# First input transfer of a dilated convolution issued from ScalarE's queue, beside the weights on SyncE's

## The chip, the cores and the metric

The kernel runs on one core of a Trainium2 chip. The metric is the device time of one execution in microseconds (us). A profiled execution gives in addition the span from the first to the last instruction, and the time of each instruction and each DMA packet. The engines are TensorE (PE, with its weight loads as PEld), VectorE (DVE), ScalarE (ACT), GpSimd (POOL) and SyncE (SP); transfers are issued from SyncE's and ScalarE's instruction queues and carried by 16 DMA engines. In the profile, q1 is the DMA queue that SyncE issues to and q10 the one that ScalarE issues to.

## What is computed

A 3x3 convolution with dilation 2 over 16 images of 64 channels, 64 by 64, to 128 output channels, zero padded so that the output is 64 by 64 too.

```python
x_pad = np.pad(x, ((0, 0), (0, 0), (2, 2), (2, 2)))
for kh in range(3):
    for kw in range(3):
        output[b, co] += weight[co, ci, kh, kw] * x_pad[b, ci, kh*2:kh*2+64, kw*2:kw*2+64]
```

Inputs, weights and output are float32: 16.8 MB of input, 0.3 MB of weights and 33.6 MB of output.

## The kernel before

The work goes by pairs of images. A pair has the 64 channels of one image on partitions 0 to 63 and those of the other on 64 to 127, so an input tile (`x32`, line 64) is 128 partitions by 4096 elements. There are eight pairs, and each is worked off in four groups of 16 output rows: 32 groups in all, in one order written out by hand (the loop over `G`).

Row blocks are combined before they are multiplied, so that fewer products are needed: in each group TensorE makes three sets of matmuls (line 173), `psP` from sums of rows (`xs`), and `psA` and `psB` from the rows themselves (`x16`, half precision), against five kinds of weights that are prepared from the three rows of the filter. A group has 6 + 12 + 12 matmuls. ScalarE then copies `psP` out of PSUM (`p_sb`, line 225), and VectorE adds it to `psA` and to `psB` (line 232) into the output tile `osb`.

Around these, by line:

- **Loads.** `load` (line 61 on) makes a tile of three buffers and issues its transfers (line 64). At the start SyncE issues the weights (line 88, 288 KB), then pair 0 in two pieces, rows 0 to 33 (1088 KB) and rows 34 to 63 (960 KB), then pairs 1 and 2 whole (2048 KB each). The loads of pairs 3 to 7 are issued by ScalarE, each after the last cast of the pair whose buffer it takes.
- **Weights.** When they have landed, VectorE, GpSimd and ScalarE make the five kinds (`wd`, lines 111 to 115). TensorE turns them with an identity matrix (line 124), and VectorE and ScalarE copy them out of PSUM as `w_sb` (lines 134 to 148). In ScalarE's queue stand, in this order: the copy to `wd` (113), the copy of kind 1 (136), the cast of rows 0 to 7 of pair 0 (146), the copy of kind 3 (147), then `casts(0)`: three casts of pair 0 (line 73: rows 18 to 33, 34 to 49, 50 to 63) and the load of pair 3, and then the first copy of `psP` (225). VectorE casts rows 8 to 17 (143) after its copy of kind 2 (138).
- **Dummies.** Ten matmuls on zeros (line 101) are placed between the steps of the preparation.
- **PSUM.** `psP` has one buffer, so the `psP` of the second group begins when the first has been copied out. `psA` and `psB` share three.
- **Stores.** SyncE issues them (line 186), each image of a pair on its own: pairs 0 and 7 in halves of 32 rows (1024 KB each, eight in all), pairs 1 to 6 whole (2048 KB, twelve in all). `osb` has three buffers, so pair n writes where pair n-3 stood, once its stores have landed.

```python
    w32 = wpool.tile([CO, CI * KH * KW], f32, name="w32")
    nc.sync.dma_start(out=w32, in_=weight.rearrange("o i h w -> o (i h w)"))
    load(0, (0, 2 * GR + d, H))
    load(1)
    load(2)
```

Here `GR` is 16, `d` is 2 and `H` is 64. Tiles and their waits are handled by the framework; the order of instructions on each engine is that of the code. The functions, with the line numbers of the profile:

Of the kernel before, what the change touches and what calls it, by code (L numbers as in the profile page):

```python
# [10 lines left out]
def kernel(  # L11
# [7 lines left out]
    nc = tc.nc  # L19

    B, CI, H, W = x.shape
# [5 lines left out]
    d = 2  # L27
# [8 lines left out]
    GR = 16  # L36
# [17 lines left out]
    x_pair = x.rearrange("(nb two) c h w -> nb (two c) (h w)", two=2)  # L54
# [4 lines left out]
    x32_tiles, x16_tiles, xs_tiles, o_tiles = {}, {}, {}, {}  # L59

    def load(pb, cuts=(0, H), queue=nc.sync):
        x32_tiles[pb] = fpool.tile([P, HW], f32, tag="x32", name="x32")
        for lo, hi in zip(cuts[:-1], cuts[1:]):
            queue.dma_start(  # L64
                out=x32_tiles[pb][:, lo * W : hi * W], in_=x_pair[pb, :, lo * W : hi * W]
            )
# [18 lines left out]
        nc.vector.tensor_tensor(out=s, in0=v[:, :, 0], in1=v[:, :, 1], op=add)  # L85

    w32 = wpool.tile([CO, CI * KH * KW], f32, name="w32")
    nc.sync.dma_start(out=w32, in_=weight.rearrange("o i h w -> o (i h w)"))  # L88
    load(0, (0, 2 * GR + d, H))
    load(1)  # L90
    load(2)
    zero = wpool.tile([P, 512], f16, name="zero")
# [26 lines left out]
    def turn(k):  # L119
# [24 lines left out]
        out=x16_tiles[0][:, 8 * W : 18 * W], in_=x32_tiles[0][:, 8 * W : 18 * W]  # L144
# [46 lines left out]
    for G in range(ngroups):  # L191
# [39 lines left out]
        for e, ps in ((0, psA), (1, psB)):  # L231
            nc.vector.tensor_tensor(  # L232
                out=o[:, :, b0 : b0 + NBLK, e],
# [49 lines left out]
```

## Time and profile before

| what | value |
|---|---|
| time, median of 8 runs | 127.63 us (127.17 to 128.65) |
| the profiled execution | 127.69 us, span 125.9 us |
| PE busy | 105.5 us (84%) |
| DVE busy | 90.5 us (72%) |
| ACT busy | 65.0 us (52%) |
| moved by DMA | 50.78 MB, mean 403 GB/s over the span |
| DMA time of SyncE's queue (q1) | 75.7% of 16 engines' span |
| DMA time of ScalarE's queue (q10) | 19.9% of 16 engines' span |
| instruction fetches (q8) | 8 packets, 0.13 MB |

The page lists each transfer that is issued, with its size and the median time from issue to landing. For the start of the kernel these lines matter (columns: what, engine, count, KB each, us to landing):

```profile
x<-in_x_dram SPq DMA_DIRECT2D x2, 2048.0 KB, 17.2
x<-in_x_dram SPq DMA_DIRECT2D x1, 1088.0 KB, 5.5
x<-in_x_dram SPq DMA_DIRECT2D x1, 960.0 KB, 7.3
w<-in_weight_dram SPq DMA_DIRECT2D x1, 288.0 KB, 2.9
```

A busy share is an average over the span. Matmuls are pipelined, so a busy PE is not one at its peak. In the slices of the span each digit is a share in tenths, and a slice is 3.15 us long. A line of the timeline gives start, length, engine, source line, operation, the tiles written and read, and in brackets how long the engine stood idle before it and who released it.

### The profile page before, as it was taken

Reading aid. Unit: us, or ns where it says so; the run is one execution under the profiler, and the core shown is the slowest. Engines: PE = TensorE matmul, PEld = TensorE weight load, DVE = VectorE, ACT = ScalarE, POOL = GpSimd, SP = SyncE. Lnnn points to the kernel's source line nnn. Section 1 sums busy time; section 2 is a strip of 40 time slices with the busy share of each in tenths; the row PEclk is TensorE's granted clock in tenths of the full one; section 3 lists DMA queues with packets and bytes.
Section 4 is the critical chain, followed back from the end, with each engine's and each line's share of the span. In section 5 each row is a group of like instructions: output and inputs, shape, how many; then the busy total and the mean of one; then the engine's idle time right before and its main releaser. Section 6 shows DMA issues by size and latency. Waiting matters only on the chain.

```text
span 125.9 us, 2336 instructions
## 1 busy us (share of the span) xinstructions
PE 105.5 (84%) x1000; PEld 54.1 (43%) x1000; DVE 90.5 (72%) x103; ACT 65.0 (52%) x68; POOL 2.2 (2%) x8
## 2 busy tenths in 40 slices
PE   6994999999999999999999995999999999900000
PEld 2251555555555555555555552445444444400000
DVE  0560998988898888988988827999888988740000
ACT  4287794366656665666666665566666533300000
POOL 2400000000000000000000000000000000000000
PEclk9999999999999999999999999999999999997555
DMA  4999999999999999999999999999999999999960
GB/s 134 374 439 427 442 422 390 390 424 409 427 432 437 427 432 432 435 416 411 427 435 432 427 427 427 432 427 442 427 416 432 427 427 442 427 393 432 432 273 26
DMA packets 4330, 50.78 MB, mean 403 GB/s; under 512 B 480, under 2 KB 480, under 8 KB 736
## 3 DMA queue, kind: packets, MB, share of 16 engines
q1 hardware_dynamic: 3600, 40.14, 75.7%
q10 hardware_dynamic: 720, 10.49, 19.9%
q8 instruction: 8, 0.13, 0.4%
q14 instruction: 2, 0.02, 0.0%
HBM read 17.07 MB, written 33.55 MB: 402 GB/s over the span
## 4 chain that ended last, share of the span: by engine, by line
PE 76%; DMA 6%; DVE 2%; ACT 2%; issue 1%; DVEq 1%; SPq 1%; ACTq 0%
PE psA L173 30%; PE psB L173 29%; PE psP L173 16%; DMA x<-in_x_dram 6%; DVE osb L232 2%; DVEq L278 1%; ACT p_sb L225 1%; ACT x L73 1%; SPq L64 0%; ACTq L64 0%; SPq L88 0%; DVEq L232 0%
## 5 line engine op out<-in xcount | busy, mean ns | idle before, releaser
L173 PEld LDWEIGHTS <-w_sb 64*128 64x128 f16 x960 | 52.0, 94 | 51.0 <-issue 3.9
L225 ACT COPY p_sb<-psP 128x1024 f32<-128x1024 f32 x32 | 32.4, 1012 | 39.3 <-PE psP L173 20.1
L232 DVE TENSOR_TENSOR osb<-psA,p_sb 128x1024 f32<-128x1024 f32 x32 | 39.2, 1224 | 16.3 <-PE psA L173 11.7
L173 PE MATMUL psB<-x,w_sb 64*128 64x496 f16 (+3 forms) x384 | 44.9, 365 | 1.4 <-DVE osb L232 1.4
L173 PE MATMUL psA<-x,w_sb 64*128 64x496 f16 (+3 forms) x384 | 44.9, 365 | 0.1
L232 DVE TENSOR_TENSOR osb<-psB,p_sb 128x1024 f32<-128x1024 f32 x32 | 39.1, 1220 | 0.0
L73 ACT CAST x<-x 128x1024 f16<-128x1024 f32 (+2 forms) x31 | 32.1, 1044 | 0.4 <-DMA x<-in_x_dram 0.4
L173 PE MATMUL psP<-xs,w_sb 64*128 64x496 f16 (+1 forms) x192 | 25.9, 371 | 1.9 <-ACT p_sb L225 1.9
L85 DVE TENSOR_TENSOR xs<-x 128x512 f16<-128x512 f16 x32 | 13.3, 416 | 0.7 <-ACT x L73 0.7
L101 PE MATMUL dm<-zero 128*128 128x512 f16 x10 | 4.6, 578 | 1.2 <-DVE zero L93 1.2
L111 DVE CAST wd<-w 128x192 f16<-128x192 f32 x1 | 0.5, 505 | 2.5 <-DMA w<-in_weight_dram 2.5
L101 PEld LDWEIGHTS <-zero 128*128 128x128 f16 x10 | 1.0, 122 | 2.7 <-issue 1.3
L124 PEld LDWEIGHTS <-wd 128*64 128x64 f16 x30 | 1.0, 118 | 2.3 <-DVE wd L111 1.2
L124 PE MATMUL wt<-ident,wd 128*64 128x128 f16 x30 | 1.6, 241 | 0.3 <-DVE wd L111 0.3
L113 ACT ACT_TABLE_LOAD x1 | 1.3, 1283 | 0.7 <-PEq L264 0.7
L136 ACT CAST w_sb<-wt 128x384 f16<-128x384 f32 x1 | 0.5, 479 | 1.9 <-PE wt L124 1.9
L113 ACT CAST wd<-w 128x192 f16<-128x192 f32 x1 | 0.5, 542 | 1.6 <-DMA w<-in_weight_dram 1.6
L138 DVE CAST w_sb<-wt 128x384 f16<-128x384 f32 x1 | 0.6, 558 | 0.9 <-PE wt L124 0.9
L93 DVE MEMSET zero<- 128x256 uint32 x1 | 0.3, 272 | 0.9 <-PEq L264 0.9
L112 POOL TENSOR_TENSOR wd<-w 128x192 f16<-128x192 f32 x1 | 0.8, 799 | 2.4 <-DMA w<-in_weight_dram 2.4
L115 POOL CAST wd<-w 128x192 f16<-128x192 f32 x1 | 0.8, 809 | 0.0
L114 DVE TENSOR_TENSOR wd<-w 128x192 f16<-128x192 f32 x1 | 0.8, 792 | 0.0
(11 smaller groups left out, 3.6 us busy)
## 6 DMA issues: line engine op xcount, KB each, us to landing
out_dram<-osb SPq DMA_DIRECT2D x12, 2048.0 KB, 18.9
x<-in_x_dram ACTq DMA_DIRECT2D x5, 2048.0 KB, 15.2
out_dram<-osb SPq DMA_DIRECT2D x8, 1024.0 KB, 14.7
x<-in_x_dram SPq DMA_DIRECT2D x2, 2048.0 KB, 17.2
x<-in_x_dram SPq DMA_DIRECT2D x1, 1088.0 KB, 5.5
x<-in_x_dram SPq DMA_DIRECT2D x1, 960.0 KB, 7.3
w<-in_weight_dram SPq DMA_DIRECT2D x1, 288.0 KB, 2.9
```

Of the source, the lines that this page charges most:

```text
L73: nc.scalar.copy(out=x16_tiles[pb][:, lo * W : hi * W], in_=x32_tiles[pb][:, lo * W : hi * W])
L85: nc.vector.tensor_tensor(out=s, in0=v[:, :, 0], in1=v[:, :, 1], op=add)
L101: nc.tensor.matmul(out=dm[:, 0:512], lhsT=zero[:, 0:P], rhs=zero)
L112: nc.gpsimd.tensor_tensor(out=wdv[:, 3], in0=wv[:, 0], in1=wv[:, 1], op=sub)
L113: nc.scalar.copy(out=wdv[:, 2], in_=wv[:, 0])
L114: nc.vector.tensor_tensor(out=wdv[:, 1], in0=wv[:, 2], in1=wv[:, 1], op=sub)
L115: nc.gpsimd.tensor_copy(out=wdv[:, 4], in_=wv[:, 2])
L124: nc.tensor.matmul(out=wts[k % 3][r * CI : (r + 1) * CI, c0 + j * CO : c0 + (j + 1) * CO], lhsT=wd[:, t * CI : (t + 1) * CI], rhs=ident,)
L173: nc.tensor.matmul(out=po, lhsT=w_sb[pp, t * CO : (t + 1) * CO], rhs=rhs, start=first and j == 1, stop=last and j == 2,)
L225: nc.scalar.copy(out=p_sb, in_=psP)
L232: nc.vector.tensor_tensor(out=o[:, :, b0 : b0 + NBLK, e], in0=ps.rearrange("p (m b q) -> p m b q", m=2, q=2 * W), in1=pv, op=add,)
L278: with _tile.TileContext(nc) as tc:
```

## The change

The first piece of pair 0 (rows 0 to 33) is issued by ScalarE as its first instruction, ahead of its table load and of everything else in its queue. SyncE issues the weights, then the second piece (rows 34 to 63), then pairs 1 and 2. Sizes, tiles and all other instructions stay as they were. In the order of instructions on the engines, ScalarE has one transfer more at its head and SyncE one fewer after the weights; TensorE, VectorE and GpSimd have theirs in the same order.

```diff
     w32 = wpool.tile([CO, CI * KH * KW], f32, name="w32")
+    load(0, (0, 2 * GR + d), queue=nc.scalar)
     nc.sync.dma_start(out=w32, in_=weight.rearrange("o i h w -> o (i h w)"))
-    load(0, (0, 2 * GR + d, H))
+    nc.sync.dma_start(
+        out=x32_tiles[0][:, (2 * GR + d) * W :], in_=x_pair[0, :, (2 * GR + d) * W :]
+    )
     load(1)
     load(2)
```

## The prediction

> **What bounds the kernel now.** I read first the page's row of engines and its slices of the span, to see which resource is full.
>
> ```profile
> PE 105.5 (84%) x1000; PEld 54.1 (43%) x1000; DVE 90.5 (72%) x103; ACT 65.0 (52%) x68; POOL 2.2 (2%) x8
> DMA  4999999999999999999999999999999999999960
> GB/s 134 374 439 427 442 422 390 390 424 409 427 432 437 427 432 432 435 416 411 427 435 432 427 427 427 432 427 442 427 416 432 427 427 442 427 393 432 432 273 26
> ```
>
> TensorE is busy in most slices and idle in the last five; the DMA row is full from the second slice to the thirty-eighth. Stretches of the trace say the same more finely (columns: stretch, its length, busy time and count of PE, PEld, DVE, ACT and POOL, clock, DMA share, GB/s).
>
> ```profile
> 1.00:2.00 1.00, 0.81 (x2) 0.28 (x3) 0.13 (x1) 1.00 (x1) 0.29 (x1) 1.00 0.23 30
> 2.00:3.00 1.00, 1.00 (x4) 0.42 (x3) 0.00 (x0) 0.02 (x1) 0.00 (x0) 1.00 1.04 343
> 12.40:75.00 62.60, 62.60 (x608) 34.65 (x609) 54.47 (x60) 39.15 (x40) 0.00 (x0) 1.00 1.01 423
> 115.00:121.00 6.00, 0.00 (x0) 0.00 (x0) 0.00 (x0) 0.00 (x0) 0.00 (x0) 0.50 1.00 422
> 121.00:126.00 5.00, 0.00 (x0) 0.00 (x0) 0.00 (x0) 0.00 (x0) 0.00 (x0) 0.50 0.19 80
> ```
>
> The DMA engines start at 1.74 us (first packet record), are full from 2 us, and still empty a backlog of stores when every engine has stopped (last add ends at 111.67). Can one engine's own packets explain its whole time? Each transfer has 128 rows, one packet each, 8 on each of 16 engines. Median packet: weights (2304 bytes) 93 ns, first piece (8704) 328, second (7680) 291, a 16384-byte row 611, an 8192-byte row 309. Per engine: 8 x (93 + 328 + 291) = 5.7; seven full loads and twelve full stores, 19 x 8 x 0.611 = 92.9; eight half stores, 64 x 0.309 = 19.8; sum 118.4 us. From 1.74 that ends at 120.1, and the first engine's part of the last store lands at 121.04. The last lands at 124.96, because two engines, judging by the landings, also carry the eight instruction fetches (886 to 964 ns each, four per engine is 3.7): 1.74 + 118.4 + 3.7 + 0.36 (last weights packet ended 3.28, landed 3.64) = 124.2, against 124.96. So the slowest DMA engine has at most some 0.8 us of slack in the whole run. The end is set by bytes on an engine that never runs dry.
>
> The chain of waits, next, seems to say otherwise. Columns: start, length, what.
>
> ```profile
> 1.64 7.33 DMA x<-in_x_dram
> 9.94 0.94 ACT x L73
> 10.90 0.39 ACTq L64
> 11.33 1.02 ACT p_sb L225
> 12.40 0.81 PE psP L173 x6
> 109.31 1.23 DVE osb L232
> ```
>
> It follows instructions and ends with VectorE's last add, not with the stores. Its start matters, though: TensorE stands from 10.52 to 12.40 for the first eviction (L225), which is queued on ScalarE behind two casts of rows 34 to 63. And its middle holds one stall, which shows who leads.
>
> ```profile
> 76.46 1.23 DVE L232 TENSOR_TENSOR osb<-psA,p_sb 128x1024 f32<-128x1024 f32 x1 [3.37 <-PE psA L173]
> 77.74 1.44 PE L173 MATMUL psB<-x,w_sb 64*128 64x512 f16 x12 [1.42 <-DVE osb L232]
> ```
>
> TensorE stops for 1.42 us because pair 5's output buffer is pair 2's, and pair 2's last store lands at 76.27 on the slowest DMA engine. Compute had run ahead of the stores and waits for them here: a start up to 1.4 us later is taken back at this point.
>
> **The change, part by part.** Three parts.
>
> *One issue leaves SyncE, one enters ScalarE.* SyncE's issue of 0.42 us (L64, from 1.17) goes; the second piece and pairs 1 and 2 are issued 0.47 us earlier, behind a queue that is full anyway. ScalarE issues first: 0.39 us by its own L64 row, then its table load of 1.28 us, now from about 1.1 to 2.4 instead of 0.73 to 2.01. Its next work needs the weights, at 3.66 at the earliest. Covered; uncovered it would be 0.4 us. GpSimd's queue issues nothing. No semaphore wait is added.
>
> *Start of the DMA.* The Trainium skill (DMA: Bandwidth & Descriptors, "Issuing engines are not separate DMA queues") holds that queues share the same 16 engines, so a second issuer saves only the sequencer's issue time. By that rule the gain is 0.42 us. By the rows it is nothing: the first piece's issue ended at 1.59 and its first packet came at 2.69, behind the weights on engines already full. The first packet of all stays 1.0 us after SyncE's issue at 0.74. What could shrink is the ramp: the weights' packets took 122 ns in the mean against 93, the first piece's 374 against 328, together 8 x (29 + 46) = 0.6 us. Bounds: 0.6 us less, or as much more; I take 0, since the same bytes start on the same idle engines.
>
> *The weights now share the engines.* Before, they were alone and landed at 3.64. How the queues share is seen from 24 to 30 us, where q1 carries 8192-byte rows and q10 16384-byte rows (columns: packets, MB, share):
>
> ```profile
> q10 hardware_dynamic: 114, 1.80, 70.8%
> q1 hardware_dynamic: 101, 0.75, 29.4%
> ```
>
> Packets alternate about one for one, whatever their size. The same skill page ("Queues, rings and completion order") agrees on round robin but puts some 9 to 17 descriptors in a packet; then an engine's 8 weight rows would pass as one, undelayed or behind all 8 rows of x: 0 or 8 x 0.328 = 2.6 us later. By the row, 8 pairs of 93 + 328 ns take 3.4 us: 1.74 + 3.4 + 0.36, with some ramp, is about 5.6, so +2.0 us. I take +2.0 and keep 0 and +2.7. The first piece lands near 5.7 to 6.6 (before 6.64) and no longer binds.
>
> All that hangs on the weights moves by 2.0: the wd copies 3.66 to 5.7, the casts of rows 0 to 17 from 6.66 to 8.7, first psA 7.33 to 9.3, end of the first psP 10.52 to 12.5. Queued on ScalarE behind the first wd copy: the w_sb copy, the x cast, the second w_sb copy, three casts, the load of pair 3, the eviction. Before, the last two casts waited 0.39 us for the second piece (8.97); that wait vanishes, since the piece lands as before, the bytes ahead of it being the same. So the casts end at 8.60 + 2.0 + 1.89 = 12.5, the issue of pair 3's load at 12.9, and the first eviction starts at 12.9 instead of 11.33: **+1.6 us** for TensorE (0 if the weights go first, 2.3 if x does). By the page's packets it would be 0 or 2.3.
>
> **What is late next.** TensorE runs without a gap from 12.4 to 75, so every store moves by 1.6. That costs only if a DMA engine runs dry. The tightest point is pair 1's first store, issued at 35.68. The engines finish the stores ahead of it between 38.0 and 41.1 (landings 38.31 to 41.48, less 0.36). With 1.6 us of delay and 1.0 us to the first packet it is there at 38.3: the quickest engines stand for 0.3 us, and they finish 3.9 us before the last one at the end. The slowest two finish their earlier stores at 39.6 and 41.1 and have 1.3 us or more to spare. At 76 the delay shrinks to 0.2. At 99.3, the next tight point, the quickest engines have 0.8 us of backlog beyond the 1.0; at 111.7 over 4. Sum for the slowest engine: 0. The profiled execution took 127.69, 1.8 outside its span; the median is 127.63. I forecast **127.6**.
>
> **The rivals.**
>
> *Compute sets the end.* Then +1.6 would arrive: 129.2. Against it: 10 us of full DMA after the last add, and the stall at 76. This needs two facts to be wrong; 0.03.
>
> *Slower: the new queue starts late and the DMA runs dry.* ScalarE's loads at 10.90, 36.89, 49.26 and 61.63 had their first packets at 14.46, 40.52, 52.85 and 65.42, 3.6 us or more after issue. If the first is that late too, x's packets start near 4.3, alternate with the second piece and pair 1, and land near 10.7; the cast at 6.66 slips by 4.0 and the first eviction to about 15.2, +3.9. TensorE would also stand some 4 us, and at the end its clock fell from 1.00 to 0.50 about 4.6 us after its last matmul; half clock over the 3.2 us of the first group adds up to 3.2. It decides once the delay passes 2.9: the second slowest engine, free at 39.6, then waits for 35.68 + delay + 1.0. At 3.9 it idles 1.0 and ends 0.8 after the old end: 128.4; at 7 several us later. Against it: those four issues met full engines, and this one meets idle ones, as SyncE's at 0.74 did (1.0 us to the first packet). The stall in the likeliest case is 2.3 us (3.93 to 6.2), nearer to the 1.9 at 10.52, after which the clock stood at 1.00. 0.15.
>
> *Faster: two queues fill the ramp.* Up to 0.6 us less, 127.0; a part of it, 127.3, is well possible but below what can be told. Over 0.5% needs more than the whole ramp: 0.06.
>
> *It does not do what it says:* the weights pass undelayed, compute starts as before, 127.6 again; it counts with the forecast.
>
> **How the numbers follow.** The forecast with its neighbours has 0.76, the first two rivals 0.18, the faster one 0.06. A measurement of this kernel can tell about 0.5%, 0.64 us, from no change: below 127.0 is faster, above 128.3 slower. The range goes from 127.0, the ramp gone, to 128.6, the late queue without a clock drop. The likeliest case's own range is 127.2 to 128.0.
>
> **What would show it.** Right: the weights land near 5.6, the wd copies start there, the first eviction near 12.9, the stall at 76 shrinks to about 0.2 us, the last add ends within 0.3 us of 111.7, the last store lands near 125, DMA share stays 1 from 2 to 121 us. Wrong: weights at 3.6 (then the sharing step fails, not the sum); a DMA share under 0.9 near 38 us; the first packet off 1.74; a last add over 2 us later.

## The result, and the profile after

The changed kernel takes 130.02 us in the median of 11 runs (128.79 to 130.96); the kernel before takes 127.69 us in 32 runs. The ratio is 1.0155, 95% interval 1.0127 to 1.0183: slower by 1.55%. The ratio leaves out runs more than 1.5% above the quickest of their kernel, so it is a little under the quotient of the medians. The profiled execution took 129.17 us (span 127.4), so it is one of the quicker ones; a second profile, further down, took 130.25.

The slices of the page, with the row of the granted clock this time:

```profile
PEclk9968999999999999999999999999999999975555
DMA  3999999999998999999999999999999999999981
GB/s 59 431 446 427 437 427 417 401 432 404 386 391 368 345 386 427 442 373 437 442 414 406 432 432 427 427 432 427 432 427 422 432 432 422 422 422 422 424 365 44
```

The clock is down in parts of the third and fourth slices, the DMA row has an 8 in the thirteenth (38.2 to 41.4 us), and the rates of the eleventh to the fifteenth are 345 to 391 GB/s. The same start in the timeline:

```profile
6.18 0.54 ACT L116 CAST wd<-w 128x192 f16<-128x192 f32 x1 [3.72 <-DMA w<-in_weight_dram]
6.74 0.36 PE L127 MATMUL wt<-ident,wd 128*64 128x128 f16 x6 [2.81 <-DVE wd L114]
9.10 0.85 PE L127 MATMUL wt<-ident,wd 128*64 128x128 f16 x12
10.42 1.40 PE L176 MATMUL psA<-x,w_sb 64*128 64x512 f16 x12
13.77 1.01 ACT L228 COPY p_sb<-psP 128x1024 f32<-128x1024 f32 x1 [0.88 <-PE psP L176]
```

The weights land at 6.15 us instead of 3.64, TensorE stands 2.81 us before them, its turn of twelve weight tiles takes 0.85 us instead of 0.53, and the first eviction (the copy of `psP`) starts at 13.77 instead of 11.33: 2.4 us late. It waits for `psP` now, no longer for the casts ahead of it in ScalarE's queue. In the kernel before:

```profile
6.43 0.53 PE L124 MATMUL wt<-ident,wd 128*64 128x128 f16 x12
7.33 1.29 PE L173 MATMUL psA<-x,w_sb 64*128 64x512 f16 x12
```

Stretches of the span (columns as before: length, busy time and count of PE, PEld, DVE, ACT, POOL, clock, DMA share, GB/s):

```profile
2.00:3.00 1.00, 1.00 (x4) 0.43 (x3) 0.00 (x0) 0.46 (x1) 0.00 (x0) 1.00 0.52 100
37.00:38.00 1.00, 1.00 (x13) 0.56 (x11) 1.00 (x2) 0.55 (x1) 0.00 (x0) 1.00 0.84 352
38.00:39.00 1.00, 1.00 (x14) 0.62 (x12) 0.83 (x3) 1.00 (x2) 0.00 (x0) 1.00 0.68 287
43.00:44.00 1.00, 1.00 (x12) 0.52 (x10) 1.00 (x1) 0.41 (x1) 0.00 (x0) 1.00 1.13 262
```

TensorE is busy all through 37 to 44 us, and the DMA is not: pair 1's first store is issued at 38.11 (before: 35.68), when the engines have little left. The last line shows something else: engines full, but only 262 GB/s. Packets of 16384 bytes took up to 1.2 us instead of 0.61. From the packet records I use two sums, each a mean over the 16 DMA engines, for every run: idle time from 15 to 50 us (35 us less the time of all data packets over 16, and 0 where that is below 0), and excess from 35 to 60 us (each data packet's time above the median of its size, over 16). Before: 0 and 0.22 us. After: 0.74 and 1.40. Together that is 1.9 us more, and the last store lands 1.47 us later (126.43 against 124.96). The stall at 76 us is gone, and the last add ends at 112.30, 0.6 us later: compute still had room.

### The profile page after: what moved, and what is told of

Read it like the earlier page. It is cut to its first block, busy times and chain, and to the rows that moved or that the text cites. A ratio compares the mean times of both kernels' runs of the same rounds, so it can differ in the third digit from the quotient of the medians.

```text
span 127.4 us, 2336 instructions
## 1 busy us (share of the span) xinstructions
PE 105.8 (83%) x1000; PEld 56.5 (44%) x1000; DVE 90.9 (71%) x103; ACT 64.9 (51%) x68; POOL 2.3 (2%) x8
## 4 chain that ended last, share of the span: by engine, by line
PE 80%; DMA 4%; DVE 1%; DVEq 1%; ACT 1%; issue 0%
PE psA L176 31%; PE psB L176 30%; PE psP L176 16%; DMA w<-in_weight_dram 4%; PE wt L127 2%; PE dm L104 1%; DVE osb L235 1%; DVEq L281 1%; ACT p_sb L228 1%; DVE wd L114 0%; DVEq L235 0%
## 5 line engine op out<-in xcount | busy, mean ns | idle before, releaser
L176 PEld LDWEIGHTS <-w_sb 64*128 64x128 f16 x960 | 54.0, 94 | 46.6 <-issue 1.6
L127 PE MATMUL wt<-ident,wd 128*64 128x128 f16 x30 | 2.1, 297 | 2.8 <-DVE wd L114 2.8
L141 DVE CAST w_sb<-wt 128x384 f16<-128x384 f32 x1 | 0.6, 557 | 0.8 <-PE wt L127 0.8
L151 DVE CAST w_sb<-wt 128x384 f16<-128x384 f32 x1 | 0.6, 558 | 0.4 <-PE wt L127 0.4
```

What stands on the lines that cost most here:

```text
L127: nc.tensor.matmul(out=wts[k % 3][r * CI : (r + 1) * CI, c0 + j * CO : c0 + (j + 1) * CO], lhsT=wd[:, t * CI : (t + 1) * CI], rhs=ident,)
L141: nc.vector.tensor_copy(out=t2[0], in_=t2[1])
L176: nc.tensor.matmul(out=po, lhsT=w_sb[pp, t * CO : (t + 1) * CO], rhs=rhs, start=first and j == 1, stop=last and j == 2,)
```

## The experiments

Theory A: the change makes compute start late, and a late start lets the DMA run short of work near 38 us; being the bound, it never gets that time back. Rivals: the time is lost at the start itself (theory B: two queues at once, slow first microseconds; called rival C where only the mix of the two queues is meant), or it is the clock alone.

In the table eviction, idle, excess and the first time are those of the one profiled execution; the last time is the median of all runs, and the ratio is to the kernel before, measured beside it. "Late dummies" stand just ahead of the first `psA`; the other twelve take the place of the first six.

| run | first eviction, us | idle, 15 to 50 | excess, 35 to 60 | profiled, us | median, us | ratio (95%) |
|---|---|---|---|---|---|---|
| before | 11.33 | 0 | 0.22 | 127.69 | 127.69 | 1 |
| before, pair 1 in halves | 12.39 | 0 | 0.20 | 127.88 | 127.74 | 1.000 (0.998 to 1.002) |
| changed, 12 dummies | 12.42 | 0 | 0.83 | 127.34 | 127.44 | 1.000 (0.998 to 1.003) |
| changed, 12 dummies, halves | 12.86 | 0 | 0.23 | 127.89 | 127.46 | 0.998 (0.996 to 1.000) |
| before, 12 late dummies | 12.87 | 0.03 | 0.65 | 128.16 | 128.06 | 1.004 (1.002 to 1.006) |
| changed, pair 1 in halves | 13.67 | 0 | 0.23 | 127.38 | 127.36 | 0.998 (0.997 to 1.000) |
| **changed** | 13.77 | 0.74 | 1.40 | 129.17 | 130.02 | 1.016 (1.013 to 1.018) |
| changed, four input buffers | 13.80 | 0 | 0.41 | 127.52 | 127.42 | 0.999 (0.997 to 1.000) |
| before, 16 late dummies | 14.10 | 1.17 | 1.68 | 129.93 | 129.47 | 1.016 (1.010 to 1.021) |
| changed, second profile | 15.16 | 1.70 | 1.54 | 130.25 | one run | none |
| weights second, halves | 15.19 | 0 | 0.40 | 128.73 | 128.06 | 1.004 (1.002 to 1.006) |
| weights second | 15.92 | 1.82 | 1.67 | 131.33 | 131.0 | 1.023 (1.017 to 1.028) |
| changed, small rows | 22.61 | 8.97 | not taken | 139.95 | 141.0 | 1.102 (1.097 to 1.107) |

**Late weights without a second queue.** In the kernel before, the weights are issued second.

```diff
+    load(0, (0, 2 * GR + d))
     nc.sync.dma_start(out=w32, in_=weight.rearrange("o i h w -> o (i h w)"))
-    load(0, (0, 2 * GR + d, H))
+    nc.sync.dma_start(
+        out=x32_tiles[0][:, (2 * GR + d) * W :], in_=x_pair[0, :, (2 * GR + d) * W :]
+    )
```

> The kernel before with one edit: SyncE issues the first piece of pair 0, then the weights, then the second piece. Only one queue is in use at the start, and the weights are late because the piece's packets go ahead of them (8 x 0.328 = 2.6 us per engine), not because two queues share. Theory A (late compute lets the DMA run dry near 38 us): weights land near 6.2 us, first eviction near 13.4 to 13.8, DMA share well under 1 near 38 us, time 129.2 to 130.5, as in the changed kernel. Theory B (two queues at the start, or the slow first microseconds of the DMA, cost the time): 127.5 to 128.0, like the kernel before.

131.0 us, half a microsecond above what theory A was given. The weights' copies started at 7.07, later than expected; TensorE stood 3.70 us before them and was at half clock to 13.74, and the first eviction came at 15.92. The DMA was nearly empty for two microseconds:

```profile
39.00:40.00 1.00, 1.00 (x14) 0.51 (x12) 1.00 (x2) 0.40 (x1) 0.00 (x0) 1.00 0.18 74
40.00:41.00 1.00, 1.00 (x14) 0.65 (x12) 0.83 (x3) 1.00 (x2) 0.00 (x0) 1.00 0.08 33
```

A second queue isn't needed for the loss; late weights, with the half clock that came with them, are enough. Theory B's first half, the two queues, falls here, and its second, the slow first microseconds, with the stores in halves further down.

**The clock.** In the changed kernel:

```diff
-    dummies(6)
+    dummies(12)
```

> The changed kernel with twelve dummy matmuls on zeros ahead of the weights' turn instead of six, so that TensorE does not stand from 3.9 to 6.7 us. Theory A with the clock as a part of the delay: granted clock stays at 1.00, first eviction near 13.2 to 13.3 instead of 13.77, the gap in the DMA near 38 us shrinks by some 0.5 us, time 129.2 to 129.7. If the clock is the whole of the loss: 127.7 to 128.2. Theory B: 130.0, unchanged.

127.44 us: all of the loss comes back, more than expected. The weights landed no sooner (their copies start at 6.12), but TensorE was kept at work:

```profile
6.68 0.36 PE L127 MATMUL wt<-ident,wd 128*64 128x128 f16 x6 [0.19 <-DVE wd L114]
8.29 0.53 PE L127 MATMUL wt<-ident,wd 128*64 128x128 f16 x12
12.42 1.01 ACT L228 COPY p_sb<-psP 128x1024 f32<-128x1024 f32 x1 [0.41 <-PE psP L176]
```

The turn takes 0.53 us instead of 0.85 and the eviction starts 1.35 us earlier than in the changed kernel. So late weights with a full clock (1.1 us of delay) cost nothing, and the half clock takes the delay over the edge. Taken alone, this run would fit the clock as the whole of the loss. But the clock acts through the delay and not beside it: the runs with halves and with late dummies show that.

**Packets no larger than the weights'.** The first piece is cut in four.

```diff
-    load(0, (0, 2 * GR + d), queue=nc.scalar)
+    load(0, (0, 9, 18, 27, 2 * GR + d), queue=nc.scalar)
```

> The changed kernel with the first piece cut into four transfers on ScalarE's queue (rows 0 to 8, 9 to 17, 18 to 26, 27 to 33), so that its packets are 2304, 2304, 2304 and 1792 bytes, no larger than the weights'. If queues take turns packet by packet, the weights land near 4.4 to 4.8 us instead of 6.15, and the first eviction starts near 12.0 or is set by the piece's own landing. Theory A: the DMA stays full near 38 us, time 127.5 to 128.3. Theory B (two queues at the start as such): 129.5 to 130.5.

141.0 us, a miss by far. The weights landed at 4.70, as expected from packets taking turns. But the pieces behind took turns too, with whole rows of 7680 and then 16384 bytes on the other queue:

```profile
x<-in_x_dram ACTq DMA_DIRECT2D x3, 288.0 KB, 7.6
x<-in_x_dram ACTq DMA_DIRECT2D x1, 224.0 KB, 17.1
```

The last 224 KB landed 17.1 us after issue, and the three casts waited 11.5 us for them; everything loaded was then on the chip and nothing stored, so the DMA stood still.

```profile
16.00:19.00 3.00, 0.00 (x0) 0.00 (x0) 0.00 (x0) 0.00 (x0) 0.00 (x0) 0.77 0.77 321
19.00:22.00 3.00, 0.00 (x0) 0.10 (x1) 0.42 (x1) 2.63 (x3) 0.00 (x0) 0.50 0.00 0
```

It agrees with the turns taken packet by packet, and with theory A at a much larger dose (eviction 11.3 us late, 13.5 us slower).

**Work for the DMA, start unchanged.** Pair 1's stores are issued in halves.

```diff
-        if pb in (0, npairs - 1):
+        if pb in (0, 1, npairs - 1):
```

> The changed kernel with pair 1's stores issued in halves of 32 rows, as pairs 0 and 7 have them; the start stays as it is. Half of pair 1's stores then comes some 6 us earlier, before the DMA runs out of work. Theory A: weights still land at 6.15, first eviction still at 13.8, but the DMA stays full from 30 to 50 us and the time comes back to 127.6 to 128.4. Theory B (loss at the start itself, in the first 10 us): 129.5 to 130.5, unchanged.

127.36 us. The start is as late as in the changed kernel (weights' copies at 6.03, eviction at 13.67), and near 38 us the DMA is full:

```profile
38.00:39.00 1.00, 1.00 (x14) 0.57 (x11) 0.83 (x2) 1.00 (x2) 0.00 (x0) 1.00 0.99 418
```

Nothing is lost at the start itself. The control, the same edit in the kernel before:

> The kernel before with pair 1's stores in halves of 32 rows, the control for the changed kernel with that edit (127.36). Theory A: the kernel before does not run dry near 36 us, so halves can gain next to nothing: 127.2 to 127.6. If halves of stores are a gain of their own whatever the start: below 126.5.

127.74 us, no difference: halves are no gain of their own. Its profile shows one thing more. Up to 30 us it is the kernel before, the weights' copies start at 3.75, and yet TensorE ran at half clock to 10.00 us:

```profile
8.38 2.07 PE L173 MATMUL psA<-x,w_sb 64*128 64x512 f16 x12
12.39 1.01 ACT L225 COPY p_sb<-psP 128x1024 f32<-128x1024 f32 x1 [1.56 <-PE psP L173]
```

So an execution of the old start can be 1.06 us later than the profile of the kernel before (11.33), nearly all of it by the clock. And in the kernel with the weights second:

> The kernel that issues the weights second on SyncE's queue (131.0, first eviction at 15.92), with pair 1's stores in halves of 32 rows. Theory A: the half stores come near 34.5 and 40.5 us, so the DMA no longer stops for most of 39 to 41 us; most of the 3.5 us comes back, 127.4 to 128.6. If the late start costs its time in another place too (the start itself, or the tail): 129.5 or more.

128.06 us. Of 2.25% all but 0.4% comes back, though the eviction is at 15.19. Where the 0.4% goes isn't settled.

**Delay alone.** In the kernel before, transfers untouched, twelve dummies ahead of the first psA, and sixteen in a second run.

```diff
     t4 = turn(4)
-    dummies(1)
+    dummies(12)
```

> The kernel before, its transfers untouched, with twelve dummy matmuls on zeros instead of one just ahead of the first psA: 11 x 0.215 us more, so that TensorE's first group ends near 12.9 and the first eviction starts near 13.0 instead of 11.33, a pure delay of some 1.6 us at full clock. This is the delay that the prediction gave the change. Theory A with the prediction's threshold (nothing lost below 2.9 us): 127.3 to 128.0. Theory A with an earlier threshold: 128.0 to 129.0, with a gap in the DMA near 38 us. Rival C (only the mixed start of two queues costs time): 127.3 to 127.8.

> As the run with twelve, but with sixteen dummies ahead of the first psA: 15 x 0.215 us more, first eviction near 13.8 us, which is where the changed kernel has it (13.77), with one queue at the start, the weights landing at 3.6 us and the clock up. Theory A: the DMA is short of work near 38 us and the time is 129.2 to 130.5, like the changed kernel. Rival C: 127.3 to 127.8.

The delays came out at 1.5 and 2.8 us: 128.06 and 129.47 us. With one queue, the weights at their old time and the clock up from 6.45 us on, sixteen dummies reproduce the loss of the changed kernel, with the gap:

```profile
38.00:39.00 1.00, 1.00 (x14) 0.62 (x12) 0.83 (x3) 1.00 (x2) 0.00 (x0) 1.00 0.16 66
```

Rival C falls. Twelve cost 0.4% without a gap in the mean. Slower packets came with it (19 of the 373 that started from 37 to 50 us took over 1.3 times their size's median; before, 1 of 376), but they don't settle where the 0.4% went: the changed kernel with twelve dummies at the start had 20 of 358, a larger excess, and lost nothing.

**More loads in hand.** The changed kernel with stores as they are.

```diff
-    XF = 3
+    XF = 4
...
-    xpool = ctx.enter_context(tc.tile_pool(name="xpool", bufs=3))
+    xpool = ctx.enter_context(tc.tile_pool(name="xpool", bufs=2))
...
     load(2)
+    load(3)
```

> The changed kernel with four input buffers instead of three (pair 3 is loaded at the start on SyncE's queue, each later load is issued one pair earlier; the half-precision tiles have two buffers instead of three to make room). Stores stay as in the changed kernel, so pair 1's first store still comes near 38 us after a first eviction near 13.8, but the DMA has one load of 2 MB (some 4.9 us) more in hand there. Theory A (the DMA runs out of work): share 1 from 3 to 121 us, 127.3 to 128.2. If it is the lateness of the stores themselves that costs the time: 129 to 130.5, as in the changed kernel.

127.42 us, with pair 1's first store at 38.15, as late as in the changed kernel. So it is not the lateness of the stores but the want of any work for the DMA.

```profile
38.00:39.00 1.00, 1.00 (x16) 0.60 (x12) 0.83 (x3) 1.00 (x2) 0.00 (x0) 1.00 1.05 442
```

**Both repairs.** Twelve dummies and halves:

> The changed kernel with both repairs, twelve dummies at the start and pair 1's stores in halves. Theory A: the DMA is full from 3 to 121 us with either repair, so both together give no more than one: 127.0 to 127.6. It beats the kernel before only if the changed start itself moves bytes sooner, which the profiles don't show.

127.46 us, no better than one alone. With halves, alone or together with dummies, the changed start is 0.2% ahead of the kernel before (ratios 0.9983 and 0.9981), with intervals that end at 0.9996 and 0.9999; that is too near no change to build on.

**The changed kernel again.**

> The changed kernel once more, for a second profile, since the one on record (129.17 us) is among the quickest of its runs. Theory A: weights near 6.1 us, first eviction at 13.7 or later, and more idle DMA time near 38 us in the slower execution; 129 to 130.7.

130.25 us, near the median. The clock is what sets it apart from the first profile: it came up at 13.03 us, and there to stay at 10.69.

```profile
6.83 0.53 PE L127 MATMUL wt<-ident,wd 128*64 128x128 f16 x6 [2.90 <-DVE wd L114]
10.90 2.31 PE L176 MATMUL psA<-x,w_sb 64*128 64x512 f16 x12
15.16 1.01 ACT L228 COPY p_sb<-psP 128x1024 f32<-128x1024 f32 x1 [1.80 <-PE psP L176]
```

The first psA takes 2.31 us here, 1.40 in the other profile and 1.29 before. The eviction is 1.4 us later still, and the DMA's share from 39 to 40 us is 0.08.

## Why the prediction was wrong

**The bound** was right: bytes on DMA engines set the end. With work in hand, a start 2.4 us late costs nothing (halves, four buffers), as argued. The likeliest outcome was built on that, and it didn't hold because the work ran out.

**The sharing of the queues** was right in kind. Packets alternate one for one: from 3 to 5 us 80 rows of the weights and 71 of the first piece started. The weights came 2.5 us late where 2.0 was taken (kept: up to 2.7). The difference is ramp: their packets took 161 ns in the mean against 122 before, and from 2 to 3 us only 100 GB/s moved. By 10 us the DMA was only 0.17 us behind the kernel before, close to the 0 that was taken.

Two steps failed, and it took both to leave the range: the delay was larger than forecast, and the delay that is free was smaller.

**The clock** made the delay larger. The prediction said of the stall: "The stall in the likeliest case is 2.3 us (3.93 to 6.2), nearer to the 1.9 at 10.52, after which the clock stood at 1.00." All of the first group was then moved by the weights' 2.0 us at its old durations, with nothing for the clock. The stall was 2.81 us, and TensorE was at half clock after it. Two errors: half a microsecond of late weights, and a row read wrongly, since the pause before the first eviction came after dense matmuls and the new one after six dummies.

Moreover, the clock is not up to begin with. In every profile here the first dummies start 0.43 us apart, and 0.22 apart once the clock is up. The changes of the clock on record lie 3.41 us or a whole multiple of it apart (in the first profile of the changed kernel 3.41, 3.41 and 102.4; before, 109.2). Stretches cut at these changes:

```profile
3.86:7.28 3.42, 0.61 (x9) 0.31 (x8) 1.10 (x2) 0.54 (x1) 1.05 (x2) 1.00 1.02 426
7.28:10.69 3.41, 3.41 (x30) 1.56 (x30) 2.15 (x6) 2.02 (x4) 0.49 (x1) 0.50 1.05 445
```

TensorE was busy for 0.61 us of the first stretch, and the second is at half clock. In the kernel before, in steps of 3.41 us from its change at 5.69, the pause at 10.52 lies in a stretch (9.10 to 12.52) with 1.54 us of work, and the clock stayed up. This agrees with the Trainium skill (TensorE: Matmul & The Clock Gate, "Part 1: The HAM clock gate"), which tells of a free-running window of about 3.4 us, and of a clock set by how busy TensorE was, so that the same kernel differs from run to run. A pause under 3.4 us was enough.

How the windows fall is luck, but late weights make it worse: the clock came up to stay at 10.30 to 13.74 us in the six profiles with six dummies in which the weights' copies start after 6 us. With twelve dummies it came up at 5.48 and 6.38, and with the weights at their old time at 5.57, 5.69, 6.45 and, in the kernel before with halves, 10.00. The profile of the kernel before, from which the prediction worked, is one with an early clock. The price of the half clock in the changed kernel: evictions at 13.77 and 15.16 against 12.42 with the dummies, so 1.35 and 2.7 us. The delay was thus 2.4 to 3.8 us and not 1.6. The rival "slower" had this price in it, but hung on a late start of the queue, which did not happen: its first packet came at 2.13 us, 1.4 after issue.

**The threshold** was too generous: "It decides once the delay passes 2.9". This is shown apart from the clock, by late dummies in the kernel before: a delay of 1.5 us cost 0.4% and one of 2.8 us 1.6%. The profiled execution of the changed kernel, at 2.4, is 1.2% above the median of before (129.17 / 127.69). With the right delay of 2.4 the sum would still have said nothing lost; with the right threshold and 1.6 us, the time would have been near the 128.06 of twelve late dummies, inside the range. The sum looked only at when the slowest engines run dry. In the kernel before, the slowest ended pair 0's last store at 41.48, in the changed one at 40.15, so over a microsecond of the slack was not there; and it had no term for the slower packets that came when pair 1's stores and the next load met a nearly empty DMA (34 of 329 in the changed kernel, 45 of 304 with sixteen dummies, 3 of 496 with four buffers). That term, 1.2 us over the kernel before, is larger than the gap's 0.74, but how much of it reaches the end isn't shown: 0.6 us of it cost nothing with twelve dummies at the start.

**Still open** is why those packets are slow. They follow the gap where there is one, and come without one too (20 of 358 with twelve dummies at the start); nothing here separates a cause.

## What to carry to other kernels

In a kernel bound by its transfers, average shares say little about where it is weak: lay issued bytes against moved bytes over time, and look for the moment with the least in hand. A delay elsewhere is free only as long as it is shorter than that backlog, less the time from issue to first packet, with something to spare. And before two transfers are put side by side, compare their row sizes: here the one with small rows was slowed by the large rows of the other (2304 bytes beside 8704: 2.5 us later).

## What was not expected of the hardware

The granted clock reads 1.00 in the second profile of the changed kernel from 7 to 11 us, while a turn of twelve took 0.85 us and the first psA 2.31, as at half clock; where no change of clock is recorded yet, durations tell more than the clock column. Four small-row transfers beside 16384-byte rows moved so slowly that the last 224 KB took 17.1 us. And the same start of a kernel had its first eviction at 11.33 us in one profile and at 12.39 in another, nearly all of it by the clock. That cost nothing there; the half clock together with late weights cost 1.55%.
